# A fused attention and recurrence kernel: tiles padded so that matrix operands start at multiples of 512 bytes

## The chip, the cores and the metric

The kernel runs on one core of a Trainium2 chip. Times are microseconds of device time of one execution; the time of a kernel is the median of its runs. Engines are called PE (TensorE), DVE (VectorE), ACT (ScalarE), POOL (GpSimd) and SP (SyncE, which issues DMAs). SBUF has 128 partitions; an address is a byte offset within a partition, the same in all 128.

## What is computed

One block of a sequence model on 1024 frames of width 1024, with 16 learned tokens put in front. The cut reference:

```
h = concat(meta, x)                                  # 16 + 1024 rows
u = rmsnorm(h, norm_g)
proj = u @ w_in                                      # 1024 -> 6144 columns
sb_q, sb_k, sb_v, sb_gate, hg_q, hg_f, hg_i, hg_gate, gate_sb, gate_hg = split(proj)
y_sb = stick_breaking(sb_q, sb_k, sb_v) * silu(sb_gate)          # 8 heads of 64, causal
y_hg = group_rmsnorm(hgrn2(hg_q, hg_f, hg_i, lb)) * silu(hg_gate)  # 4 heads of 128
merged = sigmoid(gate_sb) * (y_sb @ w_sb_out) + sigmoid(gate_hg) * (y_hg @ w_hg_out)
out = rmsnorm(h + merged @ w_out, final_norm_g)[16:]
```

Stick-breaking attention weighs an earlier position by sigmoid of its score times the product of (1 - sigmoid) over the positions between. HGRN2 is a gated linear recurrence, computed here in halves of growing length.

## The kernel before

Precision: each float32 operand is split into a high part, rounded to the matmul's input format (`F32R`), and the rest, a low part. A product is three matmuls accumulated in PSUM: high by high, high weights by low data, low weights by high data. So weights come as `wh`/`wl` (or the two halves of a `pw` tile) and data as `uh`/`ul` (the normalised rows, transposed: 8 chunks of 128 channels by 1040 columns, the first 16 of them the learned tokens).

The stages, in the order of PE's work:

- Start (to about 53 us of the span). Rows of x are loaded, normalised, transposed and split into `uh`/`ul`, in an order written out by hand. The sums of quadrants that the next stage wants are formed into `th1..th4` (high) and `tl1..tl4` (low), each 4 chunks by 512 columns. The first four projections run through line 350 and line 259.
- Seven products (about 65 to 277 us, line 466). Eleven pairs of 128-column projections are computed by a scheme with seven products in place of eight. For each pair `prep` adds and subtracts weight quadrants (`su`), splits them (ACT line 454, POOL line 455) into one of seven `pw` slots, and `product` issues 12 matmuls of 512 columns: 4 chunks by 3 parts. The list `ORDER` gives the data operand of each: w11 takes `U11`, s2 takes sum 2, s1 sum 1, s3 sum 3, w12 `U21`, s4 `U22`, w22 sum 4. `U11`, `U21`, `U22` are views of `uh`/`ul` that start at column 16 (`NM`) or 528. Weights are prepared seven products ahead.
- Attention (about 306 to 580 us) and recurrence (about 580 to 730 us). Attention's scores (line 626) are made in pieces of 144 to 456 columns, its transposes at lines 650 and 670, its value products (line 684, 256 columns) in fours. Between these, `interleave` puts projections from `stream`: groups cut into quanta of three matmuls at line 259. Key, value and forget projections take the pieces `FULL` = (0, 348), (348, 346), (694, 346) of columns; gates take `REAL` = (16, 512), (528, 512).
- The end (about 730 to 886 us). Branch products (`branch_group`, line 259, 12 matmuls a piece: 4 chunks by 3 parts of 512 columns) run group after group, while DVE and ACT split `w_out` into `BH`/`BL` (in the space of `uh`/`ul`) and other tiles. Then 28 output products at line 1316, again by seven in place of eight, with the additions and the last norm.

Tiles are handed out in a pool by tag: a tag has as many buffers as `BUFS` says, each as long as the longest tile of that tag, and buffers lie behind one another in the order in which tags are first used, at multiples of 32 bytes. Tiles of a later phase take the space of a phase that is closed. Lowest in SBUF is a scratch for descriptors of software-made DMAs, 16384 bytes, then four small constants, `ident` (512 bytes), `mhalf`, five `s4`, `uh`, `ul`, three `sg`, `wr`, `wh`, `wl` and a few small ones, then the sums `th`/`tl`, then what the phases put there. All DMAs of the kernel are issued from SP and ACT.

Of the kernel before, what the change touches and what calls it, by code (L numbers as in the profile page):

```python
# [9 lines left out]
F32R = mybir.dt.float32r  # L10
# [5 lines left out]
P = 128  # L16
D = 1024
NC = D // P
SEQ = 1024
NM = 16  # L20
L = SEQ + NM
NB = SEQ // P
EPS = 1e-6
# [7 lines left out]
HT = 512  # L31
# [4 lines left out]
    0, 512, 1024, 1536, 2048, 2560, 3072, 3584, 4096, 5120)  # L36
REAL = [(NM, 512), (NM + 512, 512)]
FULL = [(0, 348), (348, 346), (694, 346)]
QUART = [(0, 256), (256, 256), (512, 256), (768, 272)]
N_GS = 6  # L40
WS = 456
# [4 lines left out]
def block_kernel(ctx: ExitStack, tc: tile.TileContext, x, meta, norm_g, w_in, w_sb_out,  # L46
                 w_hg_out, w_out, hg_norm_g, hg_lb_logits, final_norm_g, out):
    nc = tc.nc
# [6 lines left out]
    def nm(s):  # L55
        uid[0] += 1
        return f"{s}_{uid[0]}"
# [7 lines left out]
    def sb(tag, shape, dt=F32):  # L65
        p = base if tag in HOME else here[-1]
        return p.tile(shape, dt, tag=tag, name=nm(tag), bufs=BUFS.get(tag, 1))

    def ps(tag):
        return psum.tile([P, 512], F32, tag=tag, name=nm(tag), bufs=PB[tag])  # L70

    def kept(name, shape, dt=F32):
        return dram.tile(shape, dt, tag=name, name=nm(name))
# [3 lines left out]

    ident = sb("ident", [P, P])
    make_identity(nc, ident)
    mhalf = sb("mhalf", [P, 8])  # L80
    G.memset(mhalf, -0.5)
    S.activation(sb("s4", [P, 8]), mhalf, AF.Square)

# [37 lines left out]
        return h, lo  # L121


    uh = sb("uh", [P, NC, L], F32R)
    ul = sb("ul", [P, NC, L], F32R)
    ones = sb("sg", [1, P])
    V.memset(ones, 1.0)
    early = ExitStack()
# [19 lines left out]
    for b in range(NB + 1):  # L148
# [4 lines left out]
        if b == 0:  # L153
            nc.sync.dma_start(xb[:NM], meta)
            nc.sync.dma_start(xb[NM:], x[0, 0:P - NM, :])
        elif b < NB:
            nc.sync.dma_start(xb, x[0, P * b - NM:P * (b + 1) - NM, :])
        else:
            nc.sync.dma_start(xb[:NM], x[0, SEQ - NM:SEQ, :])
        xbs.append(xb)  # L160
# [74 lines left out]
    def proj(col, pieces, evac, begin=None, after=()):  # L235
        return group(w_in[0], col, NC, pieces, u_operand, evac, begin, after)
# [80 lines left out]
    def keep_raw(to):  # L317
        def ev(acc, t0, n):
            c = sb("sg", [P, 512])
            S.activation(c[:, :n], acc, AF.Copy)  # L320
            nc.scalar.dma_start(to[:, t0:t0 + n], c[:, :n])
        return ev

    kept_i = [kept(f"hi{h}", [P, L]) for h in range(4)]
    kept_f = [kept(f"hf{h}", [P, L]) for h in range(len(FIRST) - 4)]
    raw_out = [keep_raw(t) for t in kept_i + kept_f]
# [37 lines left out]
    def further_low(b, k):  # L364
# [3 lines left out]

    STEPS = dict(S=stats, r=root, D=scaled, T=turned, H=high_part, L=low_part, R=whole, w=high_w, v=low_w, P=piece, E=kept_piece, X=further,
                 Y=further_high, y=further_high_s, Z=further_low)  # L370
    with tc.manual_schedule(engines={mybir.EngineType.Activation, mybir.EngineType.DVE, mybir.EngineType.PE}):
        for step in """
# [8 lines left out]
            Z33 Z43 Z04 Z14 Z24 Z34 Z44  # L381
            """.split():
            STEPS[step[0]](*(int(n) for n in step[1:]))
    lbl = sb("lbl", [P, 2, 4])
    hgg = sb("hgg", [P, 4])
    nc.sync.dma_start(lbl, hg_lb_logits.rearrange("r (h p) -> p r h", p=P))
    nc.sync.dma_start(hgg, hg_norm_g.rearrange("o (h p) -> p (o h)", p=P))
# [120 lines left out]
    t = sb("wt", [P, 2, 2, 512], F32R)  # L508
    V.memset(t[:, :, :, 0:P].bitcast(F32), 0.0)
    wt_last = [t[:, k] for k in range(2)]  # L510
    t = sb("wt", [P, 2, 2, 512], F32R)
    wt_full = [t[:, k] for k in range(2)]
    n_full = [0]
    t = sb("wtm", [P, 2, 256], F32R)
    V.memset(t.bitcast(F32), 0.0)
    wt_meta = [t[:, k] for k in range(2)]
    t = sb("vm", [P, 2, 2, P], F32R)
    V.memset(t.bitcast(F32), 0.0)
    v_meta = [t[:, k] for k in range(2)]

    later = sb("later", [P, WS])
    G.memset(later, 0.0)
    G.affine_select(out=later[:, WS - P:], in_=later[:, WS - P:], pattern=[[-1, P]], compare_op=ALU.is_gt, fill=1.0,
                    base=0, channel_multiplier=1)
# [1 line left out]
    def pair_groups(p):  # L526
        st = {}

        def bk():
            st["k"] = [sb("stk", [P, L], F32R) for _ in range(2)]  # L530
            st["y"] = sb("y", [P, SEQ])
            nc.sync.dma_start(st["y"], kept_sg[p])

        def bv():
            st["vt"] = sb("pt", [P, L + 1])
            st["dv"] = sb("pt", [P, L + 1])
            st["ve"] = sb("ve", [P, NB])
            V.memset(st["vt"][:, 0:1], 0.0)

        def ek(acc, t0, n):  # L540
            for hh in range(2):
                r0, r1 = hh * 64, 64 - hh * 64
                kst = st["k"][hh]
                src = acc[r0:r0 + 64]
                hi = kst[r0:r0 + 64, t0:t0 + n]
                S.activation(hi, src, AF.Copy)
                V.tensor_tensor(kst[r1:r1 + 64, t0:t0 + n], src, hi.bitcast(F32), op=ALU.subtract)

        def ev(acc, t0, n):

            vt = st["vt"]
            S.activation(vt[:, t0 + 1:t0 + n + 1], acc, AF.Copy)
            V.tensor_tensor(st["dv"][:, t0:t0 + n], vt[:, t0:t0 + n], acc, op=ALU.subtract)
            if t0 + n == L:
                G.tensor_copy(st["ve"], vt[:, NM + P:NM + P + (NB - 1) * P + 1:P])

        def v_blocks(b4):
            def emit():
                if b4 == 0:
                    st["v"] = [sb("v", [P, NB, P], F32R) for _ in range(2)]  # L560
                tp = ps("tr").rearrange("p (b n) -> p b n", b=4)
                for b in range(4):
                    t0 = NM + (b4 * 4 + b) * P
                    T.transpose(tp[:, b], st["dv"][:, t0:t0 + P], ident)
                for hh in range(2):
                    src = tp[:, :, hh * 64:hh * 64 + 64]
                    hi = st["v"][hh][:, b4 * 4:b4 * 4 + 4, 0:64]
                    S.activation(hi, src, AF.Copy)
                    V.tensor_tensor(st["v"][hh][:, b4 * 4:b4 * 4 + 4, 64:128], src, hi.bitcast(F32), op=ALU.subtract)
            return (440.0, emit)  # L570

        def v_meta_block():
            vm = v_meta[p % 2]
            st["vm"] = vm
            tp = ps("tr")
            T.transpose(tp[:NM, 0:P], st["dv"][:, 0:NM], ident)
            for r0 in (0, 32):
                src = tp[:NM, 0:P].rearrange("p (h n) -> p h n", h=2)
                S.activation(vm[r0:r0 + NM, :, 0:64], src, AF.Copy)
                V.tensor_tensor(vm[r0:r0 + NM, :, 64:128], src, vm[0:NM, :, 0:64].bitcast(F32), op=ALU.subtract)  # L580

        after_v = [v_blocks(0), v_blocks(1), (110.0, v_meta_block)]
        return st, [proj(C_V + P * p, FULL, ev, bv, after_v), proj(C_K + P * p, FULL, ek, bk)]

    def queries(i, hf):
# [7 lines left out]
    class Unit:  # L593
# [4 lines left out]
        def scores(self):  # L598

            st, hh, g = self.st, self.hh, self.g  # L600
            q = []
            ns = [NM + P * (2 * g + qi + 1) for qi in range(2)]
            room = {}

            def place(qi):
                if g > 1:
                    return sb("ab", [P, L])[:, :ns[qi]]
                if qi == 0:
                    room["t"] = sb("ab", [P, L])
                o = 0 if qi == 0 else ns[0]  # L610
                return room["t"][:, o:o + ns[qi]]

            for qi in range(2):
                n = ns[qi]
                npc = -(-n // 512)
                wd0 = -(-n // (2 * npc)) * 2
                box = {}
                for c0 in reversed(range(0, n, wd0)):
                    def piece(c0=c0, qi=qi, n=n, box=box, c1=min(c0 + wd0, n)):
                        if c1 == n:  # L620
                            box["a"] = place(qi)
                        a = box["a"]
                        qt, qo = st["q", hh, g // 2], 256 * (g % 2)
                        z = ps("z")[:, :c1 - c0]
                        for k in range(2):
                            T.matmul(z, qt[:, k, qo + qi * P:qo + (qi + 1) * P], st["k"][hh][:, c0:c1],  # L626
                                     start=(k == 0), stop=(k == 1))
                        S.activation(a[:, c0:c1], z, AF.Sigmoid, scale=-1.0)  # L628
                        w = a[:, c0:c1][:, ::-1]
                        if c1 == n:  # L630
                            ins = V.tensor_tensor_scan(w, w, later[:, WS - (n - c0):][:, ::-1],  # L631
                                                       1.0, op0=ALU.mult, op1=ALU.max)
                            anchor.append(ins)
                        else:
                            V.tensor_tensor_scan(w, w, w, a[:, c1:c1 + 1], op0=ALU.mult, op1=ALU.bypass)  # L635
                        self.w[qi] = a
                    q.append((max(wd0, 256) * 2 / 2.4, piece))
            return q
# [502 lines left out]
    for h in range(4):  # L1141
        main, t = recurrence(h, heads[h][0], (None, "ab", "v", "ab")[h]) if h else (main0, tail0)
        main = main[:2] + tail + main[2:]
        tail = t + [hg_gate(h)]
        n = (0, 1, 2, 1)[h]
# [8 lines left out]
    emit_all(stream(sbg[2:4], sbg[4]) + tail)  # L1154


    BH, BL = sb("uh", [P, 4, 4, HT], F32R), sb("ul", [P, 4, 4, HT], F32R)

    def out_rows(c):
        rows = []  # L1160
# [78 lines left out]
    t = sb("wt", [P, 2, 2, 4, P], F32R)  # L1239
# [169 lines left out]
```

## Time and profile before

| what | value |
|---|---|
| median of 3 runs | 888.22 us (888.11 to 889.62) |
| the profiled execution | 887.94 us |
| its span in the profile | 885.8 us |
| PE busy, matmuls | 868.4 us, 5684 |
| DVE, ACT, POOL busy | 615.3, 433.3, 276.7 us |
| granted PE clock over the span | 0.999 |
| read from HBM, written | 71.94 MB, 25.20 MB |

The span is the part of the execution that the profile covers; the execution is 2.1 us longer. An instruction's record says when it began and how long it took; matmuls overlap one another in the array, so a matmul's own duration (about 0.39 us at 512 columns) is longer than the distance to the next one's start. The distance is what adds up. The chain of waits follows the last instruction back to what released it, and its rows merge neighbours of one line and tile.

### The profile page before, as it was taken

To read this page: it belongs to the slowest core of one execution; us is meant where nothing else is said; L and a number is where in the kernel's file an instruction comes from. 1 tells how busy PE (TensorE), PEld (TensorE's weight loads), DVE (VectorE), ACT (ScalarE), POOL (GpSimd) and SP (SyncE) were. 2 spreads that over 40 slices of the span, in tenths; PEclk is the share of its full clock that TensorE was granted. 3 is DMA by queue.
4 is the path that set the end of the run, shared out by engine and by line. 5 is a ranking of instruction groups with operands and counts; after the bars stand their busy time and mean duration, and the time that the engine had idled before them with its cause. 6 is when DMAs were issued, how large, how long until landed. Compare 5 with 4: busy or idle time off the path is not lost.

```text
span 885.8 us, 15079 instructions
## 1 busy us (share of the span) xinstructions
PE 868.4 (98%) x5684; PEld 751.1 (85%) x5684; DVE 615.3 (69%) x1072; ACT 433.3 (49%) x1014; POOL 276.7 (31%) x303
## 2 busy tenths in 40 slices
PE   7999999999999999999999999999999999999996
PEld 6998888888888998898898898889888888888885
DVE  6894445645433368789789788876754979998775
ACT  7764333433341356556556566546444566223432
POOL 1027444544452211124211133245451110005551
PEclk9999999999999999999999999999999999999999
DMA  9222443333333612321223222112321448673312
GB/s 287 68 71 92 150 154 125 107 101 118 127 109 128 174 32 84 95 63 48 84 60 96 84 85 60 48 61 97 120 84 50 146 143 270 226 220 126 95 47 96
DMA packets 90586, 98.11 MB, mean 111 GB/s; under 512 B 6017, under 2 KB 65281, under 8 KB 90514
## 3 DMA queue, kind: packets, MB, share of 16 engines
q1 hardware_dynamic: 76832, 73.78, 27.5%
q10 hardware_dynamic: 13682, 23.37, 7.1%
q8 instruction: 45, 0.74, 0.3%
q14 instruction: 27, 0.22, 0.1%
HBM read 71.94 MB, written 25.20 MB: 110 GB/s over the span
## 4 chain that ended last, share of the span: by engine, by line
PE 90%; DVE 4%; ACT 3%; issue 1%; DMA 1%; ACTq 0%; POOL 0%; DVEq 0%
PE acc L259 37%; PE acc L466 10%; PE z L466 7%; PE tr L466 7%; PE av L684 4%; PE acc L1316 4%; PE z L626 3%; PE tr L670 3%; PE z L1316 3%; PE tr L1316 3%; PE acc L350 2%; PE z L981 1%; PE av L960 1%; DVE ab L631 1%; PE z L980 1%
## 5 line engine op out<-in xcount | busy, mean ns | idle before, releaser
L259 PE MATMUL acc<-uh,wh 128*128 128x346 f32 (+2 forms) x472 | 174.1, 369 | 0.0
L259 PE MATMUL acc<-uh,wl 128*128 128x346 f32 (+2 forms) x472 | 163.8, 347 | 0.0
L259 PE MATMUL acc<-ul,wh 128*128 128x346 f32 (+2 forms) x472 | 163.5, 346 | 0.0
L120 POOL TENSOR_TENSOR wl<-wr,wh 128x256 fp32r<-128x256 f32 x92 | 78.4, 874 | 262.3 <-ACT wh L115 234.6
L259 PEld LDWEIGHTS acc<-uh,wl 128*128 128x128 f32 x472 | 88.7, 188 | 6.8
L259 PEld LDWEIGHTS acc<-uh,wh 128*128 128x128 f32 x472 | 88.9, 188 | 3.6
L259 PEld LDWEIGHTS acc<-ul,wh 128*128 128x128 f32 x472 | 89.2, 189 | 2.1
L455 POOL TENSOR_TENSOR pw<-su,pw 128x512 fp32r<-128x512 f32 x44 | 59.2, 1364 | 44.0 <-ACT pw L454 44.0
L628 ACT ACTIVATE ab<-z 128x456 f32<-128x456 f32 (+6 forms) x112 | 49.7, 448 | 28.0 <-PE z L626 27.4
L455 POOL TENSOR_TENSOR pw<-wr,pw 128x512 fp32r<-128x512 f32 x33 | 43.7, 1323 | 61.4 <-ACT pw L454 61.4
L631 DVE TENSOR_TENSOR_SCAN ab<-ab,later 128x456 f32<-128x456 f32 (+3 forms) x64 | 55.7, 872 | 5.6 <-ACT ab L628 4.9
L466 PE MATMUL acc<-th,pw 128*128 128x512 f32 x176 | 58.0, 390 | 0.0
L454 ACT ACTIVATE pw<-su 128x512 fp32r<-128x512 f32 x44 | 26.0, 626 | 61.6 <-DVE su L449 35.1
L626 PE MATMUL z<-stk,q 128*128 128x456 f32 (+6 forms) x224 | 55.4, 329 | 0.0
L635 DVE TENSOR_TENSOR_SCAN ab<-ab 128x348 f32<-128x348 f32 (+4 forms) x48 | 47.3, 986 | 8.2 <-ACT ab L628 6.3
L672 ACT ACTIVATE wt<-tr 128x384 fp32r<-128x384 f32 (+1 forms) x68 | 37.1, 547 | 19.7 <-PE tr L670 19.5
L673 DVE TENSOR_TENSOR wt<-tr,wt 128x384 fp32r<-128x384 f32 (+1 forms) x68 | 42.1, 621 | 6.4 <-ACT wt L672 5.0
L684 PE MATMUL av<-wt,v 128*128 128x256 f32 x272 | 44.3, 285 | 1.6 <-ACT sg L696 0.9
L670 PE MATMUL tr<-ident,ab 128*128 128x128 f32 x288 | 44.7, 274 | 0.4 <-DVE wt L673 0.4
L684 PEld LDWEIGHTS av<-wt,v 128*128 128x128 f32 x272 | 39.2, 188 | 5.6 <-ACT sg L696 2.9
L115 ACT ACTIVATE wh<-wr 128x256 fp32r<-128x256 f32 x92 | 34.4, 412 | 18.8 <-PE acc L259 16.8
L626 PEld LDWEIGHTS z<-stk,q 128*128 128x128 f32 x224 | 38.7, 189 | 3.7
(425 smaller groups left out, 2081.7 us busy)
## 6 DMA issues: line engine op xcount, KB each, us to landing
wr<-in_w_in SPq DMA_DIRECT2D x48, 512.0 KB, 4.1
q<-q SPq DMA_DIRECT2D x32, 256.0 KB, 4.6
wr<-in_w_out SPq DMA_DIRECT2D x16, 512.0 KB, 4.3
sg<-gate SPq DMA_DIRECT2D x24, 256.0 KB, 3.4
gate<-sg ACTq DMA_DIRECT2D x20, 256.0 KB, 2.0
xb<-in_x SPq DMA_DIRECT2D x7, 512.0 KB, 7.9
gate<-co ACTq DMA_DIRECT2D x12, 256.0 KB, 2.0
pt<-hi SPq DMA_DIRECT2D x4, 520.0 KB, 3.5
```

The costliest lines, as they stand in the source:

```text
L120: eng.tensor_tensor(lo[:, cs], raw[:, cs], h[:, cs].bitcast(F32), op=ALU.subtract)
L259: T.matmul(acc, a, b, start=(k == 0), stop=(k == total - 1))
L455: G.tensor_tensor(t[:, 1], d[key], t[:, 0].bitcast(F32), op=ALU.subtract)
L466: T.matmul(acc, t[:, part // 2, c], (bh, bl, bh)[part][:, c], start=(c == part == 0), stop=(c == 3 and part == 2))
L626: T.matmul(z, qt[:, k, qo + qi * P:qo + (qi + 1) * P], st["k"][hh][:, c0:c1], start=(k == 0), stop=(k == 1))
L628: S.activation(a[:, c0:c1], z, AF.Sigmoid, scale=-1.0)
L631: ins = V.tensor_tensor_scan(w, w, later[:, WS - (n - c0):][:, ::-1], 1.0, op0=ALU.mult, op1=ALU.max)
L635: V.tensor_tensor_scan(w, w, w, a[:, c1:c1 + 1], op0=ALU.mult, op1=ALU.bypass)
L670: T.transpose(tp[:, c:c + P], self.w[qi][:, s0:s0 + P], ident)
L673: V.tensor_tensor(wt[:, 1, lo:], tp[:, lo:], wt[:, 0, lo:].bitcast(F32), op=ALU.subtract)
L684: T.matmul(self.av, st["v"][hh][:, 2 * gg + j], wt[:, part, where[j]:where[j] + 256], start=(gg == g and part == 0 and j == 0), stop=False)
L1316: T.matmul(a, t[:, part // 2, c], (bh, bl, bh)[part][c][:, n * HT // 2:n * HT // 2 + a.shape[-1]], start=(c == part == 0), stop=(c == 3 an ...
```

## The change

It changes where tiles lie, and the views into them; the instructions are the same. A constant `LP` = 1152 is the padded length of a row of 1040. `uh` and `ul` get 1152 columns a chunk, `ul` 16 more at its end; `mhalf` gets 128 bytes more; `lbl`, `later` and `ve` are rounded up, and `stk`, `pt` and `ab` are made of 1152 columns. `BH` and `BL` begin 16 columns into the space of `uh` and `ul`. The descriptor scratch shrinks from its default to 1024 bytes.

```
+LP = 1152
...
-    mhalf = sb("mhalf", [P, 8])
+    mhalf = sb("mhalf", [P, 8 + 32])[:, :8]
...
-    uh = sb("uh", [P, NC, L], F32R)
-    ul = sb("ul", [P, NC, L], F32R)
+    uh, ul = (sb(t, [P, NC * LP + n], F32R)[:, :NC * LP].rearrange("p (c n) -> p c n", c=NC) for t, n in (("uh", 0), ("ul", NM)))
...
-    lbl = sb("lbl", [P, 2, 4])
+    lbl = sb("lbl", [P, 96])[:, :8].rearrange("p (r h) -> p r h", r=2)
...
-    later = sb("later", [P, WS])
+    later = sb("later", [P, 512])[:, :WS]
...
-            st["k"] = [sb("stk", [P, L], F32R) for _ in range(2)]
+            st["k"] = [sb("stk", [P, LP], F32R)[:, :L] for _ in range(2)]
...
-            st["vt"] = sb("pt", [P, L + 1])
-            st["dv"] = sb("pt", [P, L + 1])
-            st["ve"] = sb("ve", [P, NB])
+            st["vt"] = sb("pt", [P, LP])[:, :L + 1]
+            st["dv"] = sb("pt", [P, LP])[:, :L + 1]
+            st["ve"] = sb("ve", [P, 64])[:, :NB]
...
-                    return sb("ab", [P, L])[:, :ns[qi]]
+                    return sb("ab", [P, LP])[:, :ns[qi]]
...
-                    room["t"] = sb("ab", [P, L])
+                    room["t"] = sb("ab", [P, LP])[:, :L]
...
-    BH, BL = sb("uh", [P, 4, 4, HT], F32R), sb("ul", [P, 4, 4, HT], F32R)
+    BH, BL = (sb(t, [P, NM + 16 * HT], F32R)[:, NM:].rearrange("p (i c n) -> p i c n", i=4, c=4) for t in ("uh", "ul"))
...
-    nc = _bacc.Bacc("TRN2", target_bir_lowering=False, num_devices=1)
+    nc = _bacc.Bacc("TRN2", target_bir_lowering=False, num_devices=1, dynamic_dma_scratch_size=1024)
```

## The prediction

> **What bounds the kernel now.** I read the head of the page first, then the chain of waits in order of time, then busy time by stage.
>
> ```profile
> span 885.8 us, 15079 instructions
> PE 868.4 (98%) x5684; PEld 751.1 (85%) x5684; DVE 615.3 (69%) x1072; ACT 433.3 (49%) x1014; POOL 276.7 (31%) x303
> PE 90%; DVE 4%; ACT 3%; issue 1%; DMA 1%; ACTq 0%; POOL 0%; DVEq 0%
> ```
>
> TensorE has 90% of the chain that ends last. Busy time of PE counts overlapping matmuls, so the pace has to be read from start to start. The chain gives it where a row holds one product of known count. This is one of the eleven rounds of the stage at line 466, in which seven products of twelve 512-wide matmuls follow each other (start, length, line, count):
>
> ```profile
> 147.87 2.75 PE z L466 x12
> 150.62 2.72 PE tr L466 x12
> 153.34 2.72 PE acc L466 x12
> 156.06 2.79 PE z L466 x12
> 158.85 2.79 PE tr L466 x12
> 161.64 5.55 PE acc L466 x24
> 167.19 2.75 PE z L466 x12
> ```
>
> All seven have the same shapes, count and order of parts, and none waits. Yet by `ORDER` the products on the sums `th`/`tl` (s2, s1, s3: the rows at 147.87, 150.62, 153.34) take 2.75, 2.72, 2.72 us, and those on `uh`/`ul` (w12, s4: 156.06, 158.85) take 2.79 each. That is 226.7 ns a matmul against 232.5. The double row holds s4's successor w22 on `th4` and the next round's w11 on `uh`: 5.55 - 2.79 = 2.76 for `th4`. Adding up the tile sizes in order of allocation shows what differs. `su`, `pw`, and all `th`/`tl` begin 480 bytes past a multiple of 512, so there moving operand and weights sit in the same place of a 512-byte block. The `uh`/`ul` operands begin at 384 + 64c for chunk c (base 320, 16 columns of lead, 4160 bytes a chunk), and their distance to the weights is never zero except by chance of one chunk. The round lasts 167.19 - 147.87 = 19.32 us.
>
> ```profile
> 64.80:277.10 212.30, 212.30 (x930) 173.88 (x930) 103.24 (x150) 78.47 (x138) 105.40 (x81) 1.00 0.37 120
> 306.00:580.00 274.00, 270.89 (x1814) 246.74 (x1813) 220.15 (x375) 161.57 (x396) 65.59 (x86) 1.00 0.24 70
> 740.00:797.00 57.00, 57.00 (x248) 46.27 (x247) 53.30 (x112) 17.88 (x38) 0.00 (x0) 1.00 0.71 230
> 797.00:876.00 79.00, 79.00 (x344) 63.85 (x343) 62.56 (x90) 28.45 (x60) 37.00 (x36) 1.00 0.26 89
> ```
>
> Columns: window, its length, then busy time and count of PE, weight loads, DVE, ACT, POOL, then the granted clock. The clock is 1.00 in all, so it does not explain two paces. In three of the stages PE is without a gap and the other engines have room; in 740 to 797 DVE has 53.30 of 57.00.
>
> **The change part by part.** No instruction is added, removed or moved, on an engine or on SP's and POOL's queues; every view keeps its shape. What changes are addresses.
>
> 1. The scratch for software-made DMA descriptors shrinks from 16384 to 1024 bytes a partition, which pays for the padding. The queues show who could miss it:
>
> ```profile
> q1 hardware_dynamic: 76832, 73.78, 27.5%
> q10 hardware_dynamic: 13682, 23.37, 7.1%
> q8 instruction: 45, 0.74, 0.3%
> q14 instruction: 27, 0.22, 0.1%
> ```
>
> There is no software queue; cost 0.
>
> 2. New addresses, by the same adding up. Constants end at 1152, `ident` at 1664, `mhalf` (160 bytes) at 1824, five `s4` at 1984: `uh` begins there, and its column 16 at 2048, a multiple of 512. Chunks are now 4608 bytes, nine blocks, so every operand of the stage at line 466 starts on a block, as `ul` and everything behind it do (the sums begin at 107008 = 209 x 512). So all seven products should run like the `th1`/`th3` rows: 7 x 2.72 = 19.04, 0.28 less a round, 11 rounds: **3.1 us**. PE has no gap there, so all of it counts. POOL works against it:
>
> ```profile
> L455 POOL TENSOR_TENSOR pw<-su,pw 128x512 fp32r<-128x512 f32 x44 | 59.2, 1364 | 44.0 <-ACT pw L454 44.0
> L455 POOL TENSOR_TENSOR pw<-wr,pw 128x512 fp32r<-128x512 f32 x33 | 43.7, 1323 | 61.4 <-ACT pw L454 61.4
> ```
>
> `su` lies in step with `pw`, `wr` does not, and the mean in step is 41 ns longer. If that is the address, 33 x 41 ns = 1.4 us are added to POOL, which is idle for half of those 212 us and prepares weights seven products ahead: hidden. Uncovered it would be a loss of 1.4.
>
> 3. The dense end. The last branch groups and the output products (`BH`, `BL`, split weights) get aligned bases too:
>
> ```profile
> 722.79 10.00 PE acc L259 x43
> 733.67 66.69 PE acc L259 x288
> 800.36 2.79 PE acc L1316 x12
> ...
> 828.22 2.83 PE acc L1316 x12
> 831.05 2.79 PE z L1316 x12
> 833.84 2.80 PE tr L1316 x12
> ...
> 875.65 1.41 PE acc L1316 x12
> ```
>
> The 288 take 231.6 ns each; at 226.7 they take 65.3: 1.4 us. From 800.36 to 875.65 are 27 products of 12, 75.29 us; at 2.72 they take 73.44: 1.85 us. The 43 go from 10.00 to 9.75: 0.25 us. Together **3.5 us**. What is late next here is DVE: with 53.30 us of work in a stretch that shrinks from 57.0 to 55.8 it has 96%, and three `acc` buffers let PE run two pieces ahead. Should DVE hold PE up, it takes back at most the 1.4 of the 288; I take 0.
>
> 4. 512-wide matmuls in short runs. Line 259 has 864 of them (10 gate groups of 48 and 16 branch groups of 24); less 288 and 43, 533 are left, mostly in quanta of three between other work. How quickly is the good pace reached? Behind the misaligned product the first `th` product takes 2.75 and `th4` 2.76, so 0.03 to 0.04 us go before 2.72 holds: at 5.8 ns each, six or seven matmuls. Runs of three never get there. Bounds: 0, and 533 x 5 ns = 2.7 us. I take **0.3 us** for the few longer runs, near the lower end by those two rows.
>
> 5. 346- and 348-wide matmuls. Their pieces start at columns 0, 348, 694, and with `uh` at 448 past a block these lie 448, 304 and 152 past one, the same for every chunk, where before the place wandered over eight. So not all operands are aligned after all.
>
> ```profile
> L259 PE MATMUL acc<-uh,wh 128*128 128x346 f32 x208 | 70.5, 339 | 0.0
> L259 PE MATMUL acc<-uh,wh 128*128 128x348 f32 x104 | 35.3, 340 | 0.0
> 280.32 13.36 PE acc L259 x84
> 296.59 12.88 PE acc L259 x81
> ```
>
> There are three parts each, 936 in all, at 159 ns. A fixed wrong place may be a little better or worse than the mean over eight. The nearest spread is that of the 1316 products, 2.76 to 2.83 around 2.79, or -2.5 to +3.3 ns a matmul: -2.3 to +3.1 us. I take 0.
>
> 6. The 256-wide value products (line 684) have weights and moving tile 96 bytes apart before, 0 after, but run in fours:
>
> ```profile
> L684 PE MATMUL av<-wt,v 128*128 128x256 f32 x272 | 44.3, 285 | 1.6 <-ACT sg L696 0.9 <-DVE sg L693 0.3
> ```
>
> By the same 5 ns at most 272 x 5 = 1.4 us gained; I take 0 by the run length, and the same size as a loss is kept for the range. Scores (pairs) and transposes (`ident` stays 128 past a block) count 0.
>
> Sum: 3.1 + 3.5 + 0.3 = 6.9 us. The profiled execution took 887.94, so 881.0; the median 888.22 stands 0.28 above it, so **881.3 us**.
>
> A rule of the Trainium skill speaks against all this. "TensorE: Matmul & The Clock Gate", Part 2, step by step, says that TensorE reads weights and moving operand through two independent ports, so that loading the next weights takes nothing from the running matmul; it gives 215.7 ns from start to start for 512 columns, at any address. By it the sum above would be 0 and the time 888.2. The trace does not agree: no product here comes under 226.7, and the same shape has two paces; so I keep the rows.
>
> **The rivals.**
>
> *A. The pace of the `th` rows has another cause than alignment* (0.15). `th` steps 2048 bytes a chunk and `uh` 4160, and the two differ in values. Against: within `th`, s2 and w22 are slow only behind a `uh` product, which looks like two streams falling into step; and the 288 end-stage matmuls, with 4096-byte tiles out of step with their weights, take 231.6. Then only the wandering of step 5 is left: 888.2, within 2 us.
>
> *B. Being at the block's very start is bad* (0.10), the slower end. In step at 480, a 512-byte weight column set crosses into the next block; at 0 both streams open the same block at once, which no row shows for a whole product. Price: the worst dense row, 2.83 for twelve. Stage 466: 77 products x (2.83 - 2.76) = 5.4 us; the end: 27 x 0.04 + (288 x 4.2 ns) = 2.3 us; 7.7 in all, 895.9. It decides where an aligned product costs over 19.32 / 7 = 2.76.
>
> *C. More than forecast* (0.09). The short runs fall into step at once, since all neighbours are aligned: 2.4 more, and 1.4 at line 684: about 877.5.
>
> *D. DVE caps the end* (0.06): the forecast less 1.4 at the 288: 882.7.
>
> The SBUF page of the Trainium skill ("SBUF — State Buffer", Who interferes with whom) says that PE waits for no other reader, which would be rival A's result; its section "Operand start alignment" adds that the runs behind it timed nothing.
>
> **How the numbers follow.** The forecast has 0.60 and its own range of 879.0 to 883.5, from steps 4 to 6. With C and D, 0.75 is faster by over 0.2% (1.8 us, about what a measurement of this kernel can tell from no change). Rival A splits: mostly within 0.2%, a little on either side. The slower 0.11 is B and a bad place of step 5 under A. The range must take in A to leave out no more than 2 in 10: 877.5 to 888.5.
>
> **What the profile of the changed kernel will show.** Right: all seven rows of a round at 2.72, a round of 19.04 us; the 288 at about 65.3; output products at 2.72; the lengths of DVE, ACT and POOL instructions as before. Step 5 is tested by the rows of 84 and 81: 13.36 and 12.88 again. Step 4: the mean pace of the gate groups between 300 and 700 us. Wrong: `uh` products still at 2.79 (A); all at 2.8 and more, `th` too (B); PE waiting for DVE between 740 and 797 (D); a new wait at 277 to 306 us, where the tiles of the attention stage take over other parts of the old tiles' space.

## The result, and the profile after

| | before | changed |
|---|---|---|
| median of 4 runs | 888.67 us (888.11 to 889.62) | 882.10 us (881.19 to 882.77) |
| profiled execution | 887.94 us | 882.37 us |
| its span | 885.8 us | 880.4 us |

The kernel before was run once more beside the changed one, so its median is 888.67 here and not 888.22. The ratio is 0.9924, with a 95% interval of 0.9907 to 0.9942: faster by 0.76%, which is 5.2 to 8.3 us by the interval. Forecast were 881.3 us and a gain of 6.9; measured were 6.6 in the medians, 5.6 between the two profiled executions, of which the spans below hold 5.4.

The head of the page after:

```profile
span 880.4 us, 15077 instructions
PE 861.4 (98%) x5684; PEld 749.6 (85%) x5684; DVE 615.1 (70%) x1072; ACT 433.4 (49%) x1014; POOL 278.1 (32%) x303
PE 81%; DVE 9%; ACT 4%; DMA 3%; issue 2%; POOL 0%; ACTq 0%; SPq 0%; DVEq 0%
```

The instructions are the same, and so are the busy times of DVE and ACT; POOL's is 1.4 us longer. PE's part of the chain has fallen from 90% to 81%, and DVE and DMA have come up: something else has got onto the path. First the round of seven products that the prediction showed (line 466 is 467 now):

```profile
146.19 2.72 PE z L467 x12
148.91 2.72 PE tr L467 x12
151.63 2.72 PE acc L467 x12
154.35 2.72 PE z L467 x12
157.07 2.72 PE tr L467 x12
159.79 5.44 PE acc L467 x24
165.23 2.72 PE z L467 x12
```

Every product takes 2.72 us, those on `uh` and those on `th` alike; the round takes 165.23 - 146.19 = 19.04 us, as worked out. Now the places where the stages meet, in the chain of before (first fence) and after (second):

```profile
34.34 5.64 PE acc L350 x48
44.28 12.08 PE acc L350 x96
67.81 2.79 PE acc L466 x12
701.41 4.36 PE acc L259 x18
```

```profile
34.34 5.46 PE acc L351 x48
44.01 11.91 PE acc L351 x96
67.30 2.73 PE acc L467 x12
276.75 13.30 PE acc L260 x84
292.94 12.80 PE acc L260 x81
697.16 4.35 PE acc L260 x18
796.37 3.01 PE acc L1317 x12
870.40 1.43 PE acc L1317 x12
```

With the rows shown in the prediction (280.32, 800.36, 875.65) these cut the span into stages:

| stage | before, us | after, us | difference | forecast |
|---|---|---|---|---|
| start, to the seven products | 67.81 | 67.30 | -0.51 | 0 |
| seven products | 212.51 | 209.45 | -3.06 | -3.1 |
| attention and recurrence | 421.09 | 420.41 | -0.68 | -0.3 |
| branch products, to the output products | 98.95 | 99.21 | +0.26 | -1.65 |
| output products | 75.29 | 74.03 | -1.26 | -1.85 |
| last additions and stores | 10.15 | 10.00 | -0.15 | 0 |

The gain of the branch products has not come. Who waits there is told by the waits of PE after (725 to 876 us; none of 0.1 us or more in the kernel before) and DVE's waits for the same tiles, before (one row) and after (two rows). Columns: in total, times, longest, us.

```profile
PE acc L260 <- DVE wh L121: 1.4, 2, 0.9
```

```profile
DVE wr L1198 <- DMA wr<-in_w_out: 1.7, 2, 1.2
```

```profile
DVE wr L1198 <- DMA wr<-in_w_out: 2.2, 1, 2.2
DVE wr L1199 <- DMA wr<-in_w_out: 2.1, 2, 1.6
```

PE waits for the low parts of the branch weights, which DVE makes; and DVE has stood 4.3 us before quarters of `w_out` that had not landed, with these low parts behind them in its program.

The two waits cost PE more than the 1.4 us in which it is idle. In PE's timeline the matmuls behind them start 0.64 and 1.03 us later than at the good pace, and the next one another 0.11 us each time: 1.9 us together, which is what lies between the forecast -1.65 and the measured +0.26. The first output products are held up too: the row at 796.37 takes 3.01 us and not 2.72, and the row behind it is as late again, which makes the 0.6 us between -1.85 and -1.26.

### The profile page after: what moved, and what is told of

Read it like the earlier page. It is cut to its first block, busy times and chain, and to the rows that moved or that the text cites. A ratio compares the mean times of both kernels' runs of the same rounds, so it can differ in the third digit from the quotient of the medians.

```text
span 880.4 us, 15077 instructions
## 1 busy us (share of the span) xinstructions
PE 861.4 (98%) x5684; PEld 749.6 (85%) x5684; DVE 615.1 (70%) x1072; ACT 433.4 (49%) x1014; POOL 278.1 (32%) x303
## 4 chain that ended last, share of the span: by engine, by line
PE 81%; DVE 9%; ACT 4%; DMA 3%; issue 2%; POOL 0%; ACTq 0%; SPq 0%; DVEq 0%
PE acc L260 28%; PE acc L467 10%; PE tr L467 7%; PE z L467 7%; PE av L685 4%; PE acc L1317 4%; PE z L627 3%; PE tr L671 3%; PE z L1317 3%; PE tr L1317 2%; PE acc L351 2%; DMA wr<-in_w_out 2%; PE av L961 1%; DVE ab L632 1%; ACT sq L170 1%
## 5 line engine op out<-in xcount | busy, mean ns | idle before, releaser
L456 POOL TENSOR_TENSOR pw<-wr,pw 128x512 fp32r<-128x512 f32 x33 | 44.1, 1335 | 60.5 <-ACT pw L455 60.5
L685 PE MATMUL av<-wt,v 128*128 128x256 f32 x272 | 44.3, 285 | 1.6 <-ACT sg L697 1.0
```

The costliest lines, as they stand in the source:

```text
L456: G.tensor_tensor(t[:, 1], d[key], t[:, 0].bitcast(F32), op=ALU.subtract)
L685: T.matmul(self.av, st["v"][hh][:, 2 * gg + j], wt[:, part, where[j]:where[j] + 256], start=(gg == g and part == 0 and j == 0), stop=False)
```

## The experiments

Theory: the pace of a stream of matmuls depends on the distance in bytes between where moving operand and weights begin, modulo a block of 512. Rivals: the descriptor scratch or lower addresses did it; each operand must start at a multiple of 512 for itself. For the end: DVE is held up by loads of `w_out`, against DVE simply having too much work.

### The scratch alone

```
-    nc = _bacc.Bacc(..., num_devices=1)
+    nc = _bacc.Bacc(..., num_devices=1, dynamic_dma_scratch_size=1024)
```

on the kernel before.

> The kernel before with the descriptor scratch cut to 1024 bytes and nothing padded. Every tile moves down by 15360 bytes, which is 30 x 512, so no operand changes its place within a 512-byte block. Theory (places within a block set the pace): the rounds of the seven products stay at 19.32 us with 2.79, 2.75, 2.72, 2.72, 2.79, 2.79, 2.76, and the time stays within 0.2% of before (888.7). Rival (the scratch, or the lower addresses, gave the gain): near 882.

888.22 us against 889.03 of before beside it, ratio 0.9991 (0.9982 to 1.0001). The chain:

```profile
153.38 2.72 PE acc L466 x12
156.10 2.79 PE z L466 x12
```

The two paces are unchanged. The scratch pays for the padding and does nothing else.

### The same distances, no multiple of 512

```
-    mhalf = sb("mhalf", [P, 8 + 32])[:, :8]
+    mhalf = sb("mhalf", [P, 8 + 32 + 16])[:, :8]
```

> The changed kernel with everything from uh on moved up by 64 bytes: moving operands and weights keep their distance of zero, but none starts at a multiple of 512 any more. Theory 1 (the distance between moving operand and weights counts): all products stay at 2.72, the time near 882. Theory 2 (each operand must start at a multiple of 512): products at 2.75 to 2.8, the time near 886 to 888.

882.63 us, ratio 0.9924 (0.9905 to 0.9942), the changed kernel's own. Its chain:

```profile
151.96 2.72 PE acc L467 x12
154.68 2.72 PE z L467 x12
```

No operand of these begins at a multiple of 512, and all run at 2.72. So it is not each operand's own place that counts here; a distance of zero is enough, and a start at multiples of 512 is one way to get it.

### Eleven distances in one kernel

```
-        t = sb("pw", [P, 2, 4, P], F32R)
+        o = (0, 8, 16, 24, 32, 48, 64, 80, 96, 112, 120)[i]
+        t = sb("pw", [P, 8 * P + P], F32R)[:, o:o + 8 * P].rearrange("p (a c n) -> p a c n", a=2, c=4)
```

> The changed kernel with the weight tiles pw moved within longer slots by a number of bytes that differs from round to round of the seven products: 0, 32, 64, 96, 128, 192, 256, 320, 384, 448, 480 in rounds 1 to 11; the data stays at multiples of 512. If the distance counts with a period of 512: round 1 at 19.04 us, the ten others at 19.3 to 19.5 (231 to 232 ns a matmul). If the period is 256 or less: the rounds at 256, or at 128 and 384 too, are at 19.04. If only the data's own place counts: all eleven at 19.04.

The chain, of each round the row of its fourth product (s3), so distances of 0, 32, 64, 96, 128, 192, 256, 320, 384, 448, 480 bytes from top to bottom:

```profile
75.51 2.72 PE acc L468 x12
...
94.79 2.80 PE acc L468 x12
...
114.39 2.80 PE acc L468 x12
...
134.01 2.81 PE acc L468 x12
...
153.62 2.79 PE acc L468 x12
...
173.03 2.75 PE acc L468 x12
...
192.19 2.72 PE acc L468 x12
...
211.47 2.80 PE acc L468 x12
...
231.03 2.79 PE acc L468 x12
...
250.60 2.80 PE acc L468 x12
...
270.20 2.80 PE acc L468 x12
```

A distance of 256 is as good as 0, and 128 and 384 are not (2.79). Most of the others are a little worse than what the kernel before had on `uh` (2.79), where the distance moved on by 64 bytes with each chunk (96, 32, 224, 160 modulo 256, in turn): a wrong distance that stays costs up to 2.81, which is 7.5 ns a matmul over the best. Only 192 and 448, 256 apart, did not agree, 2.75 and 2.80. A second kernel took other distances in another order, `(56, 112, 48, 104, 40, 88, 24, 72, 8, 64, 16)[i]` times 4 bytes.

> As the kernel with another distance in each round, with 224, 448, 192, 416, 160, 352, 96, 288, 32, 256, 64 bytes in rounds 1 to 11. The first such run gave products of 2.80 at 32 and 64, 2.81 at 96, 2.79 at 128, 2.75 at 192, 2.72 at 256, 2.80 at 320, 2.79 at 384, 2.80 at 448. If the pace depends on the distance alone: 32, 64, 96, 192, 256 and 448 come out the same here, whatever the round before. If it depends on the state that the round before left: 192, now behind 448, and 448, now behind 224, change by 0.02 or more. The period of 256 would have 192 and 448 alike, which the first run did not show.

Four of its rows, at 448, 192, 256 and 64:

```profile
94.56 2.75 PE acc L468 x12
...
113.79 2.75 PE acc L468 x12
...
250.71 2.72 PE acc L468 x12
...
269.99 2.80 PE acc L468 x12
```

192 comes out the same, and 448 takes 2.75 here where it took 2.80 in the first run. With that, the two runs agree with a period of 256: 2.72 at 0, 2.75 or 2.80 at 192, 2.79 to 2.81 at the other multiples of 32. I had put down a change at 192 or 448 as the mark of a state that is carried over from the round before; only 448 changed. The round before it was another (224, not 384), but so were the weights that it multiplies, and no run parts the two: why 448 has two paces is open. The two kernels were run once each (887.97 and 885.53 us) and serve for their rounds alone.

### Without the padding of the later stages

```
-    later = sb("later", [P, 512])[:, :WS]
+    later = sb("later", [P, WS])
...
-            st["k"] = [sb("stk", [P, LP], F32R)[:, :L] for _ in range(2)]
+            st["k"] = [sb("stk", [P, L], F32R) for _ in range(2)]
...
```

and likewise `pt`, `ve`, `ab`.

> The changed kernel without the padding of the tiles from the attention stage on (stk, pt, ab, later, ve as before): 1568 of the 2112 512-wide matmuls have a distance of zero, all of the stage at line 467 among them; in the end stage many have not. Theory: rounds at 19.04, so 3 us of the gain stay; the output products go back to 2.75 to 2.8. If the end's gain was all lost to waits for DVE anyway, the time is within 1 us of the changed kernel's; by the paces alone it is 1.5 to 2 us longer, 883.5 to 884.

884.32 us, ratio 0.9946 (0.9931 to 0.9961). The chain:

```profile
729.45 67.02 PE acc L260 x288
796.47 2.81 PE acc L1317 x12
...
821.47 2.79 PE tr L1317 x12
```

Most output products lose their gain (2.79 for 2.72). But the 288 branch matmuls, out of step and with no wait, end at 796.47, where the changed kernel, in step and waiting, ends at 796.37. So their alignment was worth nothing in the changed kernel: what the pace gained there went into the wait.

### Who holds up the end

Two ways to move work from DVE to POOL, which does nothing there. One moves the low parts of the branch weights, the other every second addition into the merged tiles.

```
-        if chunks <= NC // 2:
-            eng = V
```

> The changed kernel with the low parts of the branch weights (half-length tiles) subtracted on POOL, which does nothing from 740 to 793 us, and not on DVE: 32 subtractions of 0.42 us less for DVE. Theory (DVE, through these low weights, holds PE up at the end and ate the gain of the 288): PE's waits there go, the 288 take about 65.3 us and the time falls by 1 to 2.4 us, to about 880. Rival (the loads of w_out set the end's pace, DVE only passes it on): no gain, within 0.5 us. A third way: POOL, slower at the same subtraction and sharing DVE's port, makes the weights later still: slower by 1 us or more.

```
-                V.tensor_tensor(merged(e, t), merged(e, t), sg[:, w], op=ALU.add)
+                (V, G)[t % 2].tensor_tensor(merged(e, t), merged(e, t), sg[:, w], op=ALU.add)
```

> The changed kernel with every second addition of the recurrence branch into the merged tiles on POOL (16 additions of 0.42 us less for DVE); these feed nothing until the output products. Theory (DVE's load is what delays the low weights): PE's waits between 740 and 793 us shrink, the time falls by 0.5 to 2.4 us. Rival (the loads of w_out): no gain.

889.17 us, ratio 0.9998 (0.9989 to 1.0008), and 884.88, ratio 0.9956 (0.9943 to 0.9968). Both lose against the changed kernel. In the chain of the first (start, length) a reason can be read:

```profile
768.64 2.52 POOL wh L119
771.17 0.38 SPq L103
771.64 4.25 DMA wr<-in_w_out
```

POOL's subtractions keep the raw weights' tile; SP waits with the next load into it, and the load of `w_out` that SP issues behind it goes out late. Part of the loss is PE's clock, which went to half twice in this execution (last section). The theory's expectation failed in both, but neither run decides between the rivals, since both also delayed the loads or DVE itself (in the second, DVE was busy for 49.00 us from 740 to 793 us against 47.84 in the changed kernel, with less to do). So the loads were taken away instead:

```
-    orows = [out_rows(0)]
+    kept_rows = out_rows(0)
+    orows = [kept_rows]
...
-        orows.append(out_rows((e + 1) % 4))
+        orows.append(kept_rows)
...
-                orows.append(out_rows(e // 2 + 1))
+                orows.append(kept_rows)
```

> The changed kernel without the second to eighth load of a quarter of w_out: the first quarter's tiles are used again for all eight steps, so the output weights are others; instructions on the engines are the same. Theory (DVE, in order, stands before a quarter of w_out that has not landed, and the low branch weights behind it come late for PE): DVE's waits for w_out and PE's waits for the low weights at 754 and 788 us go, the gain of the 288 comes out, 2 to 2.4 us less: about 879.8. Rival (DVE simply has too much work there): PE still waits, the time within 0.5 us of 882.1.

879.51 us, ratio 0.9894 (0.9878 to 0.9910). In the chain:

```profile
729.10 65.30 PE acc L260 x288
```

PE has no wait left from 700 to 876 us, and the 288 take 65.30 us, the prediction's figure. DVE's work is the same (47.85 us from 740 to 793), so it was not the bound: the loads were. Without them the transfers of other tiles have more room too; the last version below keeps all loads and answers that.

### Versions that might be better

Free the tile with a quarter's upper rows first:

```
-        for i, w in enumerate((w11, w21, w22)):
-            put(i, BH[:, i, c], BL[:, i, c], w)
+        put(0, BH[:, 0, c], BL[:, 0, c], w11)
...
         put(3, BH[:, 3, c], BL[:, 3, c], w12)
+        for i, w in ((1, w21), (2, w22)):
+            put(i, BH[:, i, c], BL[:, i, c], w)
...
-        for k, w in ((2, w22), (3, w12), (4, w21)):
+        for k, w in ((3, w12), (2, w22), (4, w21)):
```

The upper rows are w11 and w12; the first edit is in `direct`, the second in `summed`.

> The changed kernel with the splits of a w_out quarter in another order, so that the tile with its upper rows is done with first and its reload can start 0.7 to 1.4 us earlier; same instructions. If late loads of w_out are what holds DVE: its waits for them (4.3 us) shrink by about 1 us each, and the time falls by 0.5 to 2 us, to about 881. If DVE's work is the bound: within 0.5 us of 882.1.

882.06 us (880.82 to 884.12), ratio 0.9923 (0.9909 to 0.9937): no measurable gain over the changed kernel. DVE's waits for `w_out` shrank from 4.3 to 3.4 us, and a load of gate values came onto the chain instead (`sg`, 4.58 us at 787.88). In this execution, which lies 1.0 us below the median, PE has no wait of 0.1 us or more among the 288, and one of 0.5 us for DVE at the first output product instead. DVE's waits:

```profile
DVE wr L1199 <- DMA wr<-in_w_out: 2.8, 2, 2.4
DVE wr L1200 <- DMA wr<-in_w_out: 0.6, 1, 0.6
```

Cut the long projections so that two pieces of three start in step:

```
-FULL = [(0, 348), (348, 346), (694, 346)]
+FULL = [(0, 272), (272, 384), (656, 384)]
```

> The changed kernel with the pieces of key, value and forget projections cut at columns 272 and 656 (272, 384, 384 wide) in place of 348 and 694: same columns in all, and two of three pieces now begin at multiples of 512. If these long rows of matmuls gain as the 512-wide ones did in dense runs (about 1 ns a matmul over the pace of now): 0.4 to 0.9 us faster, about 881.5. If runs of three gain nothing: within 0.3 us.

884.39 us, ratio 0.9945 (0.9933 to 0.9957): no gain, and rather a loss against the changed kernel. The trace shows why, and that the pieces themselves did not lose. Added up from start to start between 276 and 700 us, without PE's idle time, the matmuls of these projections took 144.6 us, against 146.0 in the changed kernel: 1.4 us gained, more than expected. But PE's idle time in this stage rose from 3.9 to 6.6 us: it got a wait in the recurrence (the row below) and two of 1.1 us for DVE in the attention (line 565), none of which the changed kernel has. What of the gain is due to places and what to the other widths was not tested.

```profile
PE z L889 <- DVE wt L925: 1.2, 1, 1.2
```

Last, the period of 256 put to use: `LP = 1088` in place of 1152, and then the space saved spent on two more `wr` buffers (`"wr": 4`).

> The changed kernel padded to multiples of 256 bytes only: a row of 1040 becomes 1088 in place of 1152 columns, 4352 bytes; of the 2112 512-wide matmuls 1626 have a distance of 0 and 486 one of 256. If distances of 0 and 256 are equally good, also mixed from chunk to chunk: rounds of 19.04 us and a time within 0.5 us of 882.1. If only a lasting distance of one kind falls into the good pace: the uh products at 2.75 to 2.8 and 1 to 2 us more.

> The same, and with the 7 KB saved two more buffers for the tag wr, which the loads of w_out go through: a quarter of w_out can be fetched while the one before is still being split. Theory (late loads of w_out held DVE, and DVE held PE): the 288 matmuls come to about 65.3 us without PE's waits, the time to about 879.7. Rival: the loads compete for the DMA engines and land as late as before: 882.

883.08 us (881.37 to 884.95), ratio 0.9934 (0.9921 to 0.9947); and 880.11 us (879.57 to 880.14), ratio 0.9894 (0.9881 to 0.9907). The first keeps the pace, with distances of 0 and 256 mixed from chunk to chunk of `uh` (a w12 product, first fence); its spread covers the changed kernel's time. The second is the best version of this study, 2.0 us below the changed kernel in the medians; the intervals of the two ratios only touch, at 0.9907. In its chain and waits (second and third fence):

```profile
154.25 2.72 PE z L467 x12
```

```profile
730.07 65.31 PE acc L260 x288
```

```profile
DVE wr L1199 <- DMA wr<-in_w_out: 0.8, 1, 0.8
```

A quarter can be fetched while the one before is split; DVE stands 0.8 us before `w_out` in place of 4.3, PE has no wait from 700 to 876 us, and the branch products give their 1.4 us.

## Why the prediction was right, and where not

- Step 1 (scratch, 0): right; the scratch alone left the time and both paces as they were.
- Step 2 (3.1 us): 3.06. Two paces for one shape inside the trace of before were the whole argument, and its reading by distance rather than by tile held: rival A fell with the `uh` products at 2.72, rival B with the pace of the `th` rows reached at multiples of 512. One detail was off: by the step's own places (weights at 480, data at 384 + 64c) the distance on `uh` was never zero, for no chunk. The price on POOL did not show: the mean of the subtractions from `wr` went from 1323 to 1335 ns, not to 1364.
- Step 3 is the one that failed. I forecast 3.5 us for the dense end and 1.0 came (1.65 + 1.85 against -0.26 + 1.26). The pace was right, as the 65.30 and 65.31 show; wrong was to take 0 for what is late next. I had looked at DVE's amount of work (96%) and bounded the loss by the 288's own 1.4 us; what held DVE was the load of `w_out` that its next instruction waited for, and PE lost 1.9 us among the branch products and 0.6 at the first output products. That was rival D's place (0.06) with another cause and a larger price.
- Step 4 (0.3) and step 5 (0): together 0.68. Added up from start to start in the two traces, the 481 matmuls of 512 columns in this stage went from 119.16 to 118.74 us, which is 0.42 for step 4, and the 863 of 346 and 348 columns from 149.16 to 148.83, which is 0.33 for step 5. The rows of 84 and 81 went from 13.36 and 12.88 to 13.30 and 12.80. Short runs gained little, as the two slow starts of the `th` rows said; rival C did not come.
- Step 6 (0): the 272 value products took 44.3 us busy before and after, although their distance went from 96 to 0.
- Not forecast: 0.51 us at the start. The 256-wide products of line 351 went from 5.64 to 5.46 and 12.08 to 11.91 us, in long runs at a distance of 448 that is now the same for every chunk. At 448 the 512-wide products took 2.75 in one of two runs, against 2.79 where the distance wandered, so the size fits; that this is the cause, and why line 684 gains nothing in step in its fours, was not tested.
- That the total came within 0.8 us of the forecast has luck in it. By the stages the forecast was 6.9 and the traces gave 5.4: the 2.5 us lost at the end were in part made up by 1.0 that was not forecast (0.51 at the start, 0.38 in attention and recurrence, 0.15 behind the output products). The medians lie 6.6 apart, and their interval takes in both figures.

The Trainium skill ("TensorE: Matmul & The Clock Gate", Part 2) says that loading the next weights takes no read bandwidth from the running matmul, and names no condition on addresses; that its pace would hold at any address was my reading. The runs with eleven distances do not bear that reading out: 2.72 to 2.81 us for twelve matmuls of one shape, with the weights moved and the data in place. What in the chip makes the distance count, no run shows.

## What to carry to other kernels

Where PE is dense, compare the start-to-start pace of equal products on different tiles: two paces in one trace can come from addresses, and their difference says what aligning may be worth. In these runs a distance of 0 or 256 bytes (modulo 512) between moving operand and weights was the best, at the price of some padding. Whether it is the addresses, a run that moves only the weights tells. A gain of 2% in PE's pace shifts a balanced stage onto whatever was nearly late: look not only at how busy the next engine is, but at what stands before the instruction that PE will need in that engine's program. Here the space that tighter padding left was worth two more buffers for what stood there.

## What the runs showed of the hardware

A dense stream of 512-wide matmuls, each with its own weights, ran at 226.7 ns from start to start when moving operand and weights began 0 or 256 bytes apart (modulo 512), and at up to 234.2 ns (2.81 us for twelve) at other distances. At a distance of 448 two paces were seen, 2.75 and 2.80 us for twelve.

In the profiled execution of the kernel with the low weights on POOL, PE stood idle for 2.0 us from 775.3 us. The windows just after it (length, then busy time and count of PE, weight loads, DVE, ACT, POOL, then the granted clock):

```profile
777.00:779.00 2.00, 1.64 (x6) 1.40 (x7) 2.00 (x5) 0.91 (x2) 0.00 (x0) 0.84 0.25 76
779.00:781.00 2.00, 2.00 (x6) 1.54 (x6) 2.00 (x4) 1.25 (x3) 0.87 (x2) 0.50 0.40 131
```

PE took up work again at 777.36 us at the full clock; the granted clock went to 0.50 about 1.0 us later, at 778.35, and came back after 3.4 us. The same followed a second idle time, of 2.2 us from 802.5 us: half clock from 805.65 to 809.07. In the kernel with the additions on POOL the granted clock stayed at 1.00 behind idle times of 1.35 and 1.72 us. So a wait of 2 us cost more than its own length: 3.4 us at half clock do 1.7 us of work, an estimate of 1.7 us lost each time. The Trainium skill, in the table "Why this matters for your kernels" of "TensorE: Matmul & The Clock Gate", warns of idle gaps above about 3 us; here 2.0 and 2.2 us were enough.
